# Turning three more things with the DMA engines in a one-core decoder step: the prompt's stick-breaking weights, its memory weights and the new sample values

## The chip, the cores and the metric

The kernel runs on one core of a Trainium2 chip. Five engines work side by side, each strictly in the order of its own queue: TensorE (PE: products; its weight loads are PEld), VectorE (DVE), ScalarE (ACT), GpSimd (POOL) and SyncE (SP), which here issues nearly all transfers to 16 DMA engines. The metric is the device time of one execution in microseconds (us), the median over several runs; lower is better.

## The reference, cut to what matters

One layer of a decoder with three branches beside each other, for 256 prompt tokens and 8 samples of 4 new tokens (288 columns in all). Two of the branches matter here, and of these the prompt's part:

```
# memory: 4 heads, 256 memory tokens
s = einsum('bqhd,bmhd->bhqm', q, k) * (HEAD_DIM ** -0.5)
p = softmax(s, axis=-1)
y = einsum('bhqm,bmhd->bqhd', p, v)
# stick-breaking: 8 heads, blocks of 128 queries, strictly causal
z = einsum('bqhd,bkhd->bhqk', q, k) * (HEAD_DIM ** -0.5) + b_sb
log_keep = where(causal, log_sigmoid(-z), 0.0)
after = cumsum(log_keep, axis=3, reverse=True) - log_keep
a = where(causal, exp(log_sigmoid(z) + after), 0.0)
y = einsum('bhqk,bkhd->bqhd', a, v)
```

The weights `p` and `a` come out with a query on each partition. The product with the values needs them with a key on each partition, so each 128x128 block is transposed ("turned") first. For two blocks of 128 queries a memory head has four such blocks; a stick-breaking head has three, as the fourth is all zeros. The samples' branch needs its new values `v` with a token on each partition: one block for each group of four heads.

## The kernel before, in words

Everything is kept with features on partitions and tokens in columns. The weights stream in as 504 slabs of 128x1024 numbers (512 KB). Each slab lands in one of four buffers `wr` (line 287), ACT rounds it to a coarse part `wh` (line 309), DVE makes the remainder `wl` (line 320), and PE multiplies: 24 products of 128x288 for a slab (line 516, in parts of six), with `wh` twice and `wl` once. `wh` and `wl` have four buffers each.

After the memory's own keys and values and the convolution's projections, PE takes the projections of the 4 memory heads and then of the 8 stick-breaking heads (key, query, values). The attention of each head is done beside these projections, as small jobs: `mem_rest(h)` for a memory head and `sb_head(h)` for a stick-breaking head. Between them they use the tile pools `s` (8 buffers of 128x512), `a` (75) and the PSUM pool `pa` (3). In `mem_rest` the scores are six products (`three`, lines 903 to 905), `softmax_rows` normalises them (line 923 last), four transposes on PE turn them (line 965), ACT and DVE split them in two parts (970, 972), and six more products with the values follow, again lines 903 to 905. In `sb_head` the scores are four products (line 1193 and `three`), a chain of ACT and DVE steps ends in the causal mask (line 1217), three transposes turn the weights (1221), ACT and DVE split them (1225, 1227, 1229), and `three` and line 1235 multiply them with the values. Each fourth head also turns `vs`, the new sample values, on PE (1187) and copies them to `vn` (1189), which `sb_sample` reads later.

One thing was turned by DMA already: the prompt's values, in `turned`. [...]

The order of all work is set before the kernel runs by a planner, `Order.run`. Each job is a Python generator that asks for an engine with an estimate (`act(n)`: 0.22 + n / 1200 us) and with what it needs: flags and buffers. The planner takes what can start earliest, and among such the smallest rank; the projections in `main` have rank 20 and fill every gap on PE. A step that changes engine is planned 0.15 us and a slack later (0.8 us for PE and SP, 0.1 us for the others). A landing is planned by `landed(kb)`: 1.2 us after the issue or after the transfers before it, then kb / 340 us, then 0.8 us. `turned` added 3.0 us to that. On the chip nothing of this is a clock: each engine works through its row as fast as the semaphores let it.

Of the kernel before, what the change touches and what calls it, by code (L numbers as in the profile page):

```python
# [75 lines left out]
class Order:  # L76
# [31 lines left out]
    def give(self, pool, n=1):  # L108
        self.pools[pool] += [self.now.ready] * n
# [49 lines left out]
def act(n, *flags, **take):  # L159
    return Ask("ACT", 0.22 + n / 1200.0, flags, **take)  # L160
# [6 lines left out]
def pe(us, *flags, **take):  # L167
    return Ask("PE", us, flags, **take)


def sp(*flags, **take):
    return Ask("SP", 0.45, flags, **take)
# [11 lines left out]
def tile_decoder_step(ctx: ExitStack, tc: tile.TileContext, xT, memT, wall, cvec, kmat, ptab,  # L184
# [23 lines left out]
    def tl(p, shape, dt=F32):  # L208
        cnt[0] += 1
        return pools[p].tile(shape, dt, tag=p, name=f"{p}_{cnt[0]}")  # L210

    def bank(p):
        return tl(p, [P, 512])
# [297 lines left out]
        done(rm_done)  # L511


    def chunk(ps, todo, first, last):
        for i, (w, a) in enumerate(todo):
            nc.tensor.matmul(ps, w, a, start=(first and i == 0), stop=(last and i == len(todo) - 1))  # L516
# [425 lines left out]
    def mem_rest(h, q):  # L942
            if h == 0:
                yield pool(1024, k4=1)
                qmx.append(tl("k4", [P, MH, NB, NS]))
                nc.gpsimd.memset(qmx[0], 0.0)
            yield dve(NS, *([qm_made[0]] if h else []))
            spread(nc, qmx[0][:, h], q[:, NP:])
            done(qm_made[h])
            qq = Pair()  # L950
            yield from split(qq, q[:, :NP], NP)
            give("a")
            yield pe(0.71, mk_done[h], *([om_made[h - 1]] if h else []), pa=1, s=1)
            s = bank("pa")
            for a in range(2):
                three(s[:, a * ML:(a + 1) * ML], qq, mk[h], slice(a * P, (a + 1) * P), slice(0, ML))
            give("a", 4)
            p = tl("s", [P, 512])
            yield from softmax_rows(s, 2, p)
            give("pa")  # L960
            yield pe(0.5, pa=1)
            tp = bank("pa")
            for m in range(2):
                for a in range(2):
                    nc.tensor.transpose(tp[:, m * NP + a * P:m * NP + (a + 1) * P],  # L965
                                        p[:, a * ML + m * P:a * ML + (m + 1) * P], ident)
            yield act(512, s=2)
            w = Pair()
            w.h, w.l = tl("s", [P, 512], F32R), tl("s", [P, 512], F32R)
            nc.scalar.copy(w.h, tp)  # L970
            yield dve(512)
            nc.vector.tensor_sub(w.l, tp, w.h.bitcast(F32))
            give("pa")
            give("s")
            yield pe(0.71, mv_done[h], pa=1)
            o = bank("pa")[:, :NP]
            for m in range(2):
                three(o, mv[h][m], w, slice((h % 2) * HD, (h % 2 + 1) * HD), slice(m * NP, (m + 1) * NP), m == 0, m == 1)
            give("s", 2)
            if h % 2:  # L980
                give("a", 4)
            yield act(NP, a=2)
            omem[h] = Acts()
            nc.scalar.copy(omem[h].h[:, :NP], o)
            yield dve(NP)
            nc.vector.tensor_sub(omem[h].l[:, :NP], o, omem[h].h[:, :NP].bitcast(F32))
            give("pa")
            done(om_made[h])
# [165 lines left out]

    def turned(h, v, vt):

        yield act(4 * P, a=1)
        x = tl("a", [P, T])[:, :NP].bitcast(U16)
        nc.scalar.copy(x.rearrange("p (x t) -> p x t", x=2), v[:, :NP].bitcast(U16).rearrange("p (t x) -> p x t", x=2))
        yield sp(a=1)  # L1160
        y = tl("a", [P, T])[:, :NP].bitcast(U16)
        nc.sync.dma_start_transpose(y.rearrange("p (c d) -> p c d", c=4), x)
        here = Flag()
        here.at = order.landed(131) + 3.0
        yield act(4 * P, here, a=1)
        f = tl("a", [P, T])
        nc.scalar.copy(f[:, :NP].bitcast(U16).rearrange("p (t x) -> p x t", x=2), y.rearrange("p (x t) -> p x t", x=2))
        give("a", 3)
        yield from split(vt, f[:, :P], P)
        vt.raw = f[:, P:NP]  # L1170
        done(v_made[h])

    def sb_head(h):
        def evac(ps):
            yield dve(T, rx_done, a=1)
            v = tl("a", [P, T])
            nc.vector.tensor_mul(v, ps, rx)
            give("pm")
            add(store(oV[h], v), 3)
            yield act(NS)  # L1180
            nc.scalar.copy(vs[:, h % 4 * NS:(h % 4 + 1) * NS], v[:, NP:])
            vt = Half()
            add(turned(h, v, vt), 2.25 + 0.05 * h)
            if h % 4 == 3:
                yield pe(0.11, pa=1)
                tp = bank("pa")[:, :P]
                nc.tensor.transpose(tp, vs, ident)
                yield act(P)
                nc.scalar.copy(vn[:, h // 4, :], tp)
                give("pa")  # L1190
            yield pe(0.54, k_made[h], q_made[h], pa=1, s=3)
            zp = bank("pa")[:, :384]
            nc.tensor.matmul(zp[:, 0:128], qs_[h].raw[:, 0:P], ks[h].raw[:, 0:P], start=True, stop=True)  # L1193
            three(zp[:, 128:384], qs_[h], ks[h], slice(0, P), slice(0, NP))
            give("a", 5)
            z, l, sp_ = (tl("s", [P, 512]) for _ in range(3))
            yield act(384)
            nc.scalar.activation(z[:, :384], zp, AF.Identity, scale=SCALE, bias=col(C_BSB + h))
            give("pa")
            zz, ll, ss = z[:, :384], l[:, :384], sp_[:, :384]  # L1200
            yield from softplus_parts(zz, ll)
            yield dve(384)
            nc.vector.scalar_tensor_tensor(ss, zz, 0.0, ll, op0=ALU.max, op1=ALU.add)
            yield dve(256)
            nc.vector.tensor_mul(blocks2(sp_, P), blocks2(sp_, P), twice(caus, P))
            yield dve(384)
            nc.vector.scalar_tensor_tensor(zz, zz, 0.0, ll, op0=ALU.min, op1=ALU.subtract)
            yield dve(2 * 384)
            nc.vector.tensor_tensor_scan(ll[:, ::-1], ones_s[:, :384][:, ::-1], ss[:, ::-1], 0.0,
                                         op0=ALU.mult, op1=ALU.add)  # L1210
            yield dve(384)
            nc.vector.tensor_sub(zz[:, :383], zz[:, :383], ll[:, 1:])
            give("s")
            yield act(384)
            act_fn(LN_EXP, zz, zz, AF.Exp)
            yield dve(256)
            nc.vector.tensor_mul(blocks2(z, P), blocks2(z, P), twice(caus, P))
            yield pe(0.35, pa=1)
            tp = bank("pa")[:, :384]
            for i in range(3):  # L1220
                nc.tensor.transpose(tp[:, i * P:(i + 1) * P], z[:, i * P:(i + 1) * P], ident)  # L1221
            yield act(256, s=2)
            w, raw = Pair(), tl("s", [P, 512])
            w.h, w.l = (lambda x: (x[:, :256], x[:, 256:]))(tl("s", [P, 512], F32R))
            nc.scalar.copy(w.h, tp[:, :256])
            yield act(P)
            nc.scalar.copy(raw[:, :P], tp[:, 256:])
            yield dve(256)
            nc.vector.tensor_sub(w.l, tp[:, :256], w.h.bitcast(F32))
            give("pa")  # L1230
            give("s", 2)
            yield pe(0.54, v_made[h], pa=1)
            op = bank("pa")[:, :NP]
            three(op, vt, w, slice(0, P), slice(0, NP), last=False)
            nc.tensor.matmul(op[:, P:NP], vt.raw, raw[:, :P], start=False, stop=True)  # L1235
            give("s", 2)
            give("a", 2)
            yield act(NP, a=2)
            a = osb[h] = Acts()
            nc.scalar.copy(a.h[:, :NP], op)  # L1240
            yield dve(NP)
            nc.vector.tensor_sub(a.l[:, :NP], op, a.h[:, :NP].bitcast(F32))
            give("pa")
            done(osb_made[h])
        return evac

    def sb_sample(g):
# [37 lines left out]
        def new_values():  # L1285
            yield pool(P, t=1)
            e = tl("t", [P, T])[:, :P]
            nc.gpsimd.memset(e, 0.0)
            for i in range(4):
                yield dve(NS)  # L1290
                c = slice(i * NS, (i + 1) * NS)
                nc.vector.transpose(e[c, c], z[c, NP:T])
            box.append(e)

        def first(ps):
            nc.tensor.matmul(ps, box[0], vn[:, g, :], start=True, stop=False)
# [384 lines left out]
```

## Time and profile before

| | |
|---|---|
| median of 3 runs | 1625.31 us (1625.14 to 1625.55) |
| profiled execution, its own time | 1625.22 us |
| its span, first to last instruction | 1623.4 us |
| busy: PE / DVE / ACT / POOL | 1618.8 / 1003.6 / 738.8 / 138.3 us |
| granted clock of PE | 1.00 |

"Busy" is the time in which an engine executed something. The profile's chain that ended last follows the work back from the last instruction; its lines say which engine and which line of the kernel held the end at each moment. Tile names are those of the pools, with numbers left out. The heads' attention lies between about 137 and 357 us of the span.

### The profile page before, as it was taken

What the parts mean: (1) busy time and instruction counts of PE and PEld (TensorE: products, weight loads), DVE (VectorE), ACT (ScalarE), POOL (GpSimd) and SP (SyncE); (2) the same over time, 40 slices, a digit from 0 to 9 for tenths busy, and PEclk for the clock granted to TensorE, in tenths of its full rate; (3) what the DMA queues carried; (4) which work ended last, traced back from release to release, by engine and by line L of the source; (5) the groups of instructions that cost most, each with busy time, mean ns of one, the idle gap of its engine ahead of it and who ended that gap; (6) DMA issues with size and microseconds to landing.
All of it is one profiled execution on the core that took longest, in us unless ns stands there. A gap on an engine that the chain in (4) does not pass through costs nothing.

```text
span 1623.4 us, 30845 instructions
## 1 busy us (share of the span) xinstructions
PE 1618.8 (100%) x12713; PEld 1603.1 (99%) x12713; DVE 1003.6 (62%) x1493; ACT 738.8 (46%) x1068; POOL 138.3 (9%) x107
## 2 busy tenths in 40 slices
PE   9999999999999999999999999999999999999999
PEld 7999999999999999999999999999999999999999
DVE  8899898877777755665555544555445544455543
ACT  8746766654433544444443333333333333333332
POOL 0020000000000000002222100121001210022100
PEclk9999999999999999999999999999999999999999
DMA  9787465788755555556655555555555555555662
GB/s 337 216 187 267 141 178 177 255 287 298 266 179 173 167 170 169 168 176 193 195 171 170 170 169 170 167 169 169 170 168 168 170 170 168 171 168 169 181 191 101
DMA packets 111454, 306.36 MB, mean 189 GB/s; under 512 B 24274, under 2 KB 33874, under 8 KB 111314
## 3 DMA queue, kind: packets, MB, share of 16 engines
q1 hardware_dynamic: 111170, 304.38, 60.0%
q8 instruction: 99, 1.62, 0.4%
q14 instruction: 41, 0.34, 0.1%
q10 hardware_dynamic: 144, 0.02, 0.0%
HBM read 296.99 MB, written 6.32 MB: 187 GB/s over the span
## 4 chain that ended last, share of the span: by engine, by line
PE 100%; POOL 0%; DVE 0%; issue 0%; POOLq 0%
PE pm L516 93%; PE pm L569 3%; PE pa L516 1%; PE pl L1070 1%; PE pl L1259 0%; PE pa L903 0%; PE pa L905 0%; PE pa L904 0%; PE pl L1084 0%; PE pa L1477 0%; PE pa L1221 0%; PE pa L1193 0%; PE pa L965 0%; PE pa L1235 0%; PE pa L863 0%; PE pa L663 0%
## 5 line engine op out<-in xcount | busy, mean ns | idle before, releaser
L309 ACT CAST wh<-wr 128x1024 fp32r<-128x1024 f32 (+1 forms) x520 | 530.4, 1023 | 633.1 <-PE pm L516 569.3
L516 PE MATMUL pm<-a,wh 128*128 128x288 f32 x5184 | 738.5, 293 | 0.0
L320 DVE TENSOR_TENSOR wl<-wr,wh 128x1024 fp32r<-128x1024 f32 (+1 forms) x520 | 620.0, 1195 | 191.1 <-ACT wh L309 187.8
L516 PEld LDWEIGHTS pm<-a,wh 128*128 128x128 f32 x5184 | 695.9, 188 | 1.0 <-issue 1.0
L516 PE MATMUL pm<-a,wl 128*128 128x288 f32 x2592 | 397.9, 292 | 0.0
L516 PEld LDWEIGHTS pm<-a,wl 128*128 128x128 f32 x2592 | 358.2, 188 | 0.2 <-issue 0.2
L516 PE MATMUL pm<-k,wh 128*128 128x288 f32 x2400 | 338.1, 292 | 0.0
L516 PEld LDWEIGHTS pm<-k,wh 128*128 128x128 f32 x2400 | 321.1, 188 | 0.0
L516 PE MATMUL pm<-k,wl 128*128 128x288 f32 x1200 | 182.1, 292 | 0.0
L516 PEld LDWEIGHTS pm<-k,wl 128*128 128x128 f32 x1200 | 165.2, 188 | 0.0
L1414 POOL TENSOR_TENSOR t<-t 128x288 f32<-128x288 f32 x64 | 95.5, 1494 | 600.5 <-DVE t L1411 600.5
L1428 DVE TENSOR_TENSOR a<-a,pm 128x288 f32<-128x288 f32 x64 | 29.1, 454 | 122.4 <-PE pm L516 122.4
L1411 DVE SCALAR_TENSOR_TENSOR t<-pm,rx 128x288 f32<-128x288 f32 x64 | 29.2, 457 | 90.8 <-PE pm L516 90.8
L1417 ACT CAST k<-t 128x288 fp32r<-128x288 f32 x60 | 25.9, 433 | 123.3 <-POOL t L1414 123.3
L1330 DVE TENSOR_TENSOR t<-pm,rx 128x288 f32<-128x288 f32 x48 | 22.0, 458 | 68.1 <-PE pm L516 68.1
L1419 DVE TENSOR_TENSOR k<-t,k 128x288 fp32r<-128x288 f32 x60 | 27.8, 465 | 58.3 <-ACT k L1417 58.3
L747 DVE SCALAR_TENSOR_TENSOR a<-a,cv,a 128x256 f32<-128x256 f32 x120 | 57.5, 480 | 1.4
L1400 POOL TENSOR_TENSOR t<-t,t 128x288 f32<-128x288 f32 x15 | 21.6, 1443 | 387.6 <-ACT t L1397 387.6
L569 PE MATMUL pm<-wh,a 128*128 128x512 f32 x128 | 35.0, 395 | 0.0
L516 PE MATMUL pm<-s,wh 128*128 128x288 f32 x160 | 33.9, 292 | 0.0
L569 PEld LDWEIGHTS pm<-wh,a 128*128 128x128 f32 x128 | 24.3, 191 | 5.7 <-ACT wh L309 0.7
L516 PEld LDWEIGHTS pm<-s,wh 128*128 128x128 f32 x160 | 25.4, 188 | 0.0
(209 smaller groups left out, 738.3 us busy)
## 6 DMA issues: line engine op xcount, KB each, us to landing
wr<-in_wall SPq DMA_DIRECT2D x488, 512.0 KB, 3.6
wr<-in_wall SPq DMA_DIRECT2D x32, 256.0 KB, 4.8
k<-in_kpool SPq DMA_DIRECT2D x32, 256.0 KB, 6.0
k<-in_vpool SPq DMA_DIRECT2D x32, 256.0 KB, 6.0
k<-in_mkc SPq DMA_DIRECT2D x8, 512.0 KB, 8.5
k<-in_mvc SPq DMA_DIRECT2D x8, 512.0 KB, 7.9
t<-in_xT SPq DMA_DIRECT2D x16, 144.0 KB, 3.5
out_yT<-a SPq DMA_DIRECT2D x16, 144.0 KB, 1.8
```

What stands on the lines that cost most here:

```text
L309: nc.scalar.copy(sl.h[:, c], sl.raw[:, c])
L320: nc.vector.tensor_sub(sl.l[:, c], sl.raw[:, c], sl.h[:, c].bitcast(F32))
L516: nc.tensor.matmul(ps, w, a, start=(first and i == 0), stop=(last and i == len(todo) - 1))
L569: nc.tensor.matmul(ps[m], y[:, m * P:(m + 1) * P], z[:, w], start=(k == 0 and j < 2), stop=(k == KT - 1 and j in (4, 5)))
L747: nc.vector.scalar_tensor_tensor(c[:, :NP], up[:, k:k + NP], w, c[:, :NP], op0=ALU.mult, op1=ALU.add)
L1330: nc.vector.tensor_mul(g, ps, rx)
L1400: nc.gpsimd.tensor_add(sq_sum[0], sq_sum[0], res[0])
L1411: nc.vector.scalar_tensor_tensor(r, ps, 0.0, r2, op0=ALU.max, op1=ALU.mult)
L1414: nc.gpsimd.tensor_mul(r, r, r)
L1417: nc.scalar.copy(a.h, r)
L1419: nc.vector.tensor_sub(a.l, r, a.h.bitcast(F32))
L1428: nc.vector.tensor_add(x1[j], x1[j], ps)
```

## The change

A helper `turn(src, n, place, ...)` takes the three steps out of `turned`: ACT writes the planes, SP issues the DMA transpose, ACT joins the halfwords. `place` names the tiles to use. It plans 2.0 us, where `turned` had 3.0 us, after the landing. It is used for four things now:

- the prompt's values, as before (4 blocks of 128x128 halfwords for a head, 8 times);
- a memory head's weights (512 numbers in a row, 8 blocks, 4 times), instead of line 965;
- a stick-breaking head's weights (384 numbers, 6 blocks, 8 times), instead of line 1221. They end in the tile `ll`, so the copy of the third block (1227) is gone too;
- the new sample values (128 numbers, 2 blocks, twice), instead of lines 1187 and 1189, in a job of their own, `turned_new`, that writes `vn`.

The splits (970, 972, 1225, 1229) then read SBUF, where they read PSUM. `sb_head(4)` is planned after `vn` of the first group, and `sb_sample` after its own.

```diff
+    def turn(src, n, place, **take):
+
+        yield act(2 * n, **take)
+        x, y, out = place()
+        nc.scalar.copy(planes(x), halves(src))
+        yield sp()
+        nc.sync.dma_start_transpose(y.bitcast(U16).rearrange("p (c d) -> p c d", d=P), x.bitcast(U16))
+        here = Flag()
+        here.at = order.landed(n * P * 4 / 1e3) + 2.0
+        yield act(2 * n, here)
+        nc.scalar.copy(halves(out), planes(y))
+        return out
...
-            yield pe(0.5, pa=1)
-            tp = bank("pa")
-            for m in range(2):
-                for a in range(2):
-                    nc.tensor.transpose(tp[:, m * NP + a * P:m * NP + (a + 1) * P],
-                                        p[:, a * ML + m * P:a * ML + (m + 1) * P], ident)
+            def place():
+                x = tl("s", [P, 512])
+                return x, p, x
+
+            x = yield from turn(p, 512, place, s=1)
+            give("s")
             yield act(512, s=2)
             w = Pair()
             w.h, w.l = tl("s", [P, 512], F32R), tl("s", [P, 512], F32R)
-            nc.scalar.copy(w.h, tp)
+            x, wh = (y.rearrange("p (i j q) -> p i j q", i=2, j=2) for y in (x, w.h))
+            wh = wh.rearrange("p m a q -> p a m q")
+            nc.scalar.copy(wh, x)
             yield dve(512)
-            nc.vector.tensor_sub(w.l, tp, w.h.bitcast(F32))
-            give("pa")
+            nc.vector.tensor_sub(w.l.rearrange("p (m a q) -> p a m q", m=2, a=2), x, wh.bitcast(F32))
...
+    def turned_new(g):
+
+        def place():
+            x, y = (tl("a", [P, T])[:, :P] for _ in range(2))
+            return x, y, vn[:, g, :]
+
+        yield from turn(vs, P, place, a=2)
+        give("a", 2)
+        done(vn_made[g])
...
             if h % 4 == 3:
-                yield pe(0.11, pa=1)
-                tp = bank("pa")[:, :P]
-                nc.tensor.transpose(tp, vs, ident)
-                yield act(P)
-                nc.scalar.copy(vn[:, h // 4, :], tp)
-                give("pa")
+                add(turned_new(h // 4), 2.9)
...
-            yield pe(0.35, pa=1)
-            tp = bank("pa")[:, :384]
-            for i in range(3):
-                nc.tensor.transpose(tp[:, i * P:(i + 1) * P], z[:, i * P:(i + 1) * P], ident)
-            yield act(256, s=2)
-            w, raw = Pair(), tl("s", [P, 512])
+            yield from turn(zz, 384, lambda: (ll, zz, ll))
+            give("s")
+            yield act(256, s=1)
+            w = Pair()
             w.h, w.l = (lambda x: (x[:, :256], x[:, 256:]))(tl("s", [P, 512], F32R))
-            nc.scalar.copy(w.h, tp[:, :256])
-            yield act(P)
-            nc.scalar.copy(raw[:, :P], tp[:, 256:])
+            nc.scalar.copy(w.h, ll[:, :256])
             yield dve(256)
-            nc.vector.tensor_sub(w.l, tp[:, :256], w.h.bitcast(F32))
-            give("pa")
-            give("s", 2)
+            nc.vector.tensor_sub(w.l, ll[:, :256], w.h.bitcast(F32))
...
-            nc.tensor.matmul(op[:, P:NP], vt.raw, raw[:, :P], start=False, stop=True)
+            nc.tensor.matmul(op[:, P:NP], vt.raw, ll[:, 256:], start=False, stop=True)
```

The planner then writes other rows for every engine. Three places are shown. Lines are those of each kernel: 516, 903 to 905, 1193 and 1235 of before are 535, 922 to 924, 1214 and 1250 of the kernel after; 524, 526 and 530 are the three steps of `turn`.

PE of before, at the transposes of stick-breaking head 0 (`km` holds the identity, `pm` is the projection under way, `wh` the slab):

```order
L516 MATMUL pm_2633<-a_282,wh_2521 128x288
L516 MATMUL pm_2633<-a_283,wh_2521 128x288
L1221 MATMUL pa_2645<-km,s_2451 128x128 x3
L516 MATMUL pm_2633<-a_378,wh_2521 128x288
L516 MATMUL pm_2633<-a_379,wh_2521 128x288
```

The three transposes stand between products of a slab. PE of before, 24 products of the projection and four transposes later, at the same head's product with its values:

```order
L516 MATMUL pm_2633<-a_607,wh_2545 128x288
L903 MATMUL pa_2700<-s_2667,a_2325 128x256
L904 MATMUL pa_2700<-s_2667,a_2325 128x256
L905 MATMUL pa_2700<-s_2667,a_2325 128x256
L1235 MATMUL pa_2700<-s_2666,a_2316 128x128
L516 MATMUL pm_2633<-a_610,wh_2545 128x288
```

PE of the kernel after, at the same product (`s_2374` is now the tile `ll`):

```order
L535 MATMUL pm_2573<-a_511,wl_2531 128x288
L535 MATMUL pm_2573<-a_544,wl_2531 128x288
L922 MATMUL pa_2667<-s_2637,a_2318 128x256
L923 MATMUL pa_2667<-s_2637,a_2318 128x256
L924 MATMUL pa_2667<-s_2637,a_2318 128x256
L1250 MATMUL pa_2667<-s_2374,a_2197 128x128
L535 MATMUL pm_2573<-a_606,wl_2531 128x288
```

Between the head's first score product and its first product with the values PE had 120 projection products in its row, and has 156 now. For memory head 3, the same count goes from 84 to 114; for the other ten heads it grows by 12 (where 64 small products of the samples come between as well) to 120.

SP of before, around the values of stick-breaking head 1 (`wr` is a slab, `out_oK` and `out_oV` are outputs):

```order
L678 DMA out_oK<-a_2357 128x288
L287 DMA wr_2417<-in_wall 128x1024
L678 DMA out_oV<-a_2441 128x288
L287 DMA wr_2466<-in_wall 128x1024
L1162 DMA_TRANSPOSE a_2481<-a_2455 128x4x128
L287 DMA wr_2523<-in_wall 128x1024
L287 DMA wr_2560<-in_wall 128x1024
```

SP of the kernel after, at the same values:

```order
L287 DMA wr_2416<-in_wall 128x1024
L697 DMA out_oV<-a_2419 128x288
L526 DMA_TRANSPOSE s_2364<-s_2437 128x8x128
L526 DMA_TRANSPOSE a_2468<-a_2467 128x4x128
L287 DMA wr_2497<-in_wall 128x1024
L287 DMA wr_2529<-in_wall 128x1024
L526 DMA_TRANSPOSE s_2373<-s_2374 128x6x128
L287 DMA wr_2549<-in_wall 128x1024
```

The weights of memory head 1 (`s_2364`) and of stick-breaking head 0 (`s_2373`) are turned on each side of the values' transpose, with slabs behind them. ACT of before, from the split of head 0's turned weights on:

```order
L1225 CAST s_2667<-pa_2645 128x256
L1227 COPY s_2666<-pa_2645 128x128
L845 ACTIVATE t_2627<-t_2626 128x288
L845 ACTIVATE t_2641<-t_2640 128x288
L309 CAST wh_2689<-wr_2523 128x1024
L970 CAST s_2705<-pa_2683 128x512
```

ACT of the kernel after, at the landing of head 0's weights:

```order
L309 CAST wh_2571<-wr_2416 128x1024
L309 CAST wh_2589<-wr_2497 128x1024
L1004 CAST a_2604<-pa_2582 128x256
L226 ACTIVATE t_2395<-pa_2594,eps 128x288
L226 ACTIVATE t_2395<-t_2395 128x288
L871 CAST t_2510<-t_2509 32x288
L530 COPY s_2374<-s_2373 128x2x384
L1244 CAST s_2637<-s_2374 128x256
```

Where ACT had waited for PE's transposes, it now waits at line 530 for a landing, and what stands behind it in its row, slabs too, waits with it.

More of the change, by code (lines that the diff above doesn't have):

```diff
@@ L511, in mem_norm, with planes, halves @@
         done(rm_done)
+    def planes(x):
+        return x.bitcast(U16).rearrange("p (x t) -> p x t", x=2)
+    def halves(x):
+        return x.bitcast(U16).rearrange("p (t x) -> p x t", x=2)
+    def turn(src, n, place, **take):
[9 more added lines that the diff above has]
+        return out
     def chunk(ps, todo, first, last):
@@ L1155, in turned, with place @@
     def turned(h, v, vt):
[L1157 to L1170, printed above, removed]
-        done(v_made[h])
+        def place():
+            x, y = (tl("a", [P, T])[:, :NP] for _ in range(2))
+            return x, y, x
+        x = yield from turn(v[:, :NP], NP, place, a=2)
+        give("a", 2)
+        yield from split(vt, x[:, :P], P)
+        vt.raw = x[:, P:]
+        done(v_made[h])
+    def turned_new(g):
+        def place():
+            x, y = (tl("a", [P, T])[:, :P] for _ in range(2))
+            return x, y, vn[:, g, :]
+        yield from turn(vs, P, place, a=2)
+        give("a", 2)
+        done(vn_made[g])
+    vn_made = [Flag(), Flag()]
     def sb_head(h):
@@ L1179, in evac @@
             add(store(oV[h], v), 3)
-            yield act(NS)
+            yield act(NS, *([vn_made[0]] if h == 4 else []))
             nc.scalar.copy(vs[:, h % 4 * NS:(h % 4 + 1) * NS], v[:, NP:])
@@ L1293, in new_values @@
             box.append(e)
+            yield dve(0, vn_made[g])
         def first(ps):
```

## Prediction

> **What bounds the kernel now.** I read the page first, its busy times and its chain of waits, then that chain in order of time around the edit, then one row of engine times over the stretch of the heads.
>
> ```profile
> span 1623.4 us, 30845 instructions
> PE 1618.8 (100%) x12713; PEld 1603.1 (99%) x12713; DVE 1003.6 (62%) x1493; ACT 738.8 (46%) x1068; POOL 138.3 (9%) x107
> ...
> PEclk9999999999999999999999999999999999999999
> ...
> PE 100%; POOL 0%; DVE 0%; issue 0%; POOLq 0%
> ```
>
> PE carries the whole chain, at full granted clock; of 1623.4 us it is busy 1618.8. So any PE instruction that goes away shortens the span by its own pitch, as long as PE never waits for what replaces it. The chain in order of time gives that pitch, since each piece there lasts until the next begins:
>
> ```profile
> 144.25 0.44 PE pa L965 x4
> ...
> 159.87 0.59 PE pa L965 x4
> ...
> 188.11 0.33 PE pa L1221 x3
> ...
> 188.44 2.35 PE pm L516 x18
> ...
> 225.98 0.11 PE pa L1187
> ...
> 352.53 0.33 PE pa L1221 x3
> ```
>
> A transpose holds PE for 0.44 / 4 = 0.33 / 3 = 0.11 us, though its own record is longer; a product of a slab holds it for 2.35 / 18 = 0.1306 us.
>
> ```profile
> core 0: us, PE busy (x) PEld busy (x) DVE busy (x) ACT busy (x) POOL busy (x), PEclk, DMA share, GB/s
> 120.00:360.00 240.00, 240.00 (x2040) 236.10 (x2040) 211.64 (x390) 158.21 (x309) 4.91 (x6) 1.00 0.66 213
> ```
>
> In the stretch of the heads PE has no gap, ACT is busy 158.2 / 240 = 66%, DVE 88%, the DMA engines 66%. So ACT and DMA have room; DVE has little, but its row keeps its work.
>
> **The change, part by part.** PE loses 4 x 4 + 8 x 3 + 2 = 42 transposes: 42 x 0.11 = 4.62 us. (The one group at 0.59 us follows small products; I count its extra 0.15 us as theirs. With it the gain is 4.77 us.) Nothing is added on PE. This is the gain, all of it on the chain.
>
> ACT and DVE are priced from these rows (min/median/max in ns):
>
> ```profile
> L1159 ACT COPY a<-a x8: 602/614/616, 153.0 to 317.8; 128x512 uint16<-128x512 uint16 x8
> L1167 ACT COPY a<-a x8: 770/778/786, 162.7 to 326.6; 128x512 uint16<-128x512 uint16 x8
> L1181 ACT COPY vs<-a x8: 202/218/219, 152.9 to 317.6; 128x32 f32<-128x32 f32 x8
> L1225 ACT CAST s<-pa x8: 349/373/375, 189.1 to 352.9; 128x256 fp32r<-128x256 f32 x8
> L1227 ACT COPY s<-pa x8: 262/272/281, 189.3 to 353.2; 128x128 f32<-128x128 f32 x8
> L970 ACT CAST s<-pa x4: 586/588/589, 144.7 to 191.3; 128x512 fp32r<-128x512 f32 x4
> L1229 DVE TENSOR_TENSOR s<-pa,s x8: 414/420/426, 189.7 to 354.4; 128x256 fp32r<-128x256 f32 x8
> L972 DVE TENSOR_TENSOR s<-pa,s x4: 682/691/693, 146.1 to 193.3; 128x512 fp32r<-128x512 f32 x4
> ```
>
> Taking 0.22 us for a nearly empty copy (L1181) as the fixed part, 512 halfwords cost 0.39 us more to spread into planes and 0.56 us more to join. So a stick-breaking head (768 halfwords) pays 0.22 + 0.59 = 0.81 and 0.22 + 0.84 = 1.06 us, a memory head (1024) 1.01 and 1.34 us, the sample values (256) 0.42 and 0.50 us. Bounds for the largest: the times at 512 as they are, or doubled (0.61 to 1.23 and 0.78 to 1.56 us). Sum: 8 x 1.87 + 4 x 2.35 + 2 x 0.92 = 26.2 us, less 8 x 0.27 for line 1227 and 2 x about 0.27 for line 1189 (same shape): +23.5 us. ACT then stands at (158.2 + 23.5) / 240 = 76% of the stretch; I cost that at nothing, since PE's products cover it. The splits read SBUF in place of PSUM; I take the same durations, and a tenth either way is under 0.1 us on a path with the reserves below.
>
> SP issues 14 more transposes, 4 x 8 + 8 x 6 + 2 x 2 = 84 more blocks. The rows of the present ones, and one that followed the samples' pages:
>
> ```profile
> L1162 SPq DMA_TRANSPOSE a<-a x8: 1197/1204/1666, 153.6 to 318.4; - x8
> ...
> DMA to landing us min/median/max: 2.4/3.9/9.2
> ...
> 295.48 0.82 SPq L1035 DMA_DIRECT2D k<-in_mvc  x1
> 296.40 1.22 SPq L1162 DMA_TRANSPOSE a<-a  x1
> ...
> 248.50:249.50 1.00, 1.00 (x10) 1.00 (x9) 0.97 (x2) 0.98 (x2) 0.00 (x0) 1.00 0.48 86
> 249.50:250.50 1.00, 1.00 (x10) 1.00 (x9) 0.96 (x3) 0.12 (x1) 0.00 (x0) 1.00 0.77 111
> ```
>
> Issuing takes 1.20 / 4 = 0.30 us a block if each block is issued for itself, 25 us over the stretch, with slabs queued behind; bound below: 1.20 us whatever the size. In the two windows at 249 us, just after a transpose was issued, the DMA engines were busy 0.48 + 0.77 = 1.25 us, an estimate of one transpose; 84 blocks make 21 x 1.25 = 26 us, out of 240 x 0.34 = 82 us that are free. I cost both at nothing: PE's products cover them.
>
> What remains is latency. From issue to landing a transpose of 4 blocks took 3.9 us (median); with 0.30 us a block I take 4.5 us for 6 blocks and 5.1 us for 8 (bounds: 2.4 us, and 9.2 us behind a backlog of pages). Does PE reach the product with the values before its operand is there? The tightest places by the order are stick-breaking head 0 and memory head 3:
>
> ```profile
> 185.90 0.42 DVE L1217 TENSOR_TENSOR s<-s,km 128x256 f32<-128x256 f32 x1
> 189.66 0.42 DVE L1229 TENSOR_TENSOR s<-pa,s 128x256 fp32r<-128x256 f32 x1
> 191.85 0.28 PE L903 MATMUL pa<-s,a 128*128 128x256 f32 x1
> ...
> 188.25 0.89 ACT L923 ACTIVATE s<-s,sm 128x256 f32<-128x256 f32 x2
> ...
> 193.29 0.68 DVE L972 TENSOR_TENSOR s<-pa,s 128x512 fp32r<-128x512 f32 x1
> ...
> 196.34 0.28 PE L903 MATMUL pa<-s,a 128*128 128x256 f32 x1
> ```
>
> Head 0: its masked weights were ready at 186.32, and PE took them at 191.85, 5.53 us later; the split had ended at 190.08, so 1.77 us of that were reserve. The new way needs 0.81 + 4.5 + 1.06 + 0.37 + 0.42 = 7.2 us and hand-overs (estimate 0.4 us). PE's row has 36 more products in between (156 for 120) and 11 transposes less, those of two memory heads and its own: 36 x 0.1306 - 11 x 0.11 = 3.5 us more. 5.53 + 3.5 = 9.0 us are there for 7.6 us, if ACT and DVE come to the mask as early as before: a landing up to 5.9 us is free. Memory head 3: 196.34 - 189.14 = 7.2 us, and 114 products for 84, 6 transposes less and three 128x256 products more (0.12 us each) make 3.5 us more, 10.7 us. Needed: 1.01 + 5.1 + 1.34 + 0.59 + 0.69 + 0.4 = 9.1 us; a landing up to 6.7 us is free. By the same count every other head gains 5.5 to 20 us of cover. So typical landings hide, and a backlogged one at a tight head would not: I allow 0.2 us in all for PE's waits. The transposes of the sample values feed a product that comes tens of us later; no cost.
>
> [...]
>
> Sum against the profiled execution: 1625.22 - 4.62 + 0.2 = 1620.8 us. The median of the runs lies 0.09 us above that execution, so 1620.9 us.
>
> **The rivals.**
>
> A. Some landings come late, and PE waits at line 1250 or at a memory head's product. For it: the 9.2 us landing above, issued right behind a page of the samples; with two more blocks 9.8 us, 3.9 us over what head 0 has. Against it: the heads behind pages (4, 6 and 7) got 16 to 20 us of cover. One such wait: 1620.7 + 3.9 = 1624.6 us; two: 1628.5 us. It takes the gain back to within 0.2% (1622.1) from 1.4 us on.
>
> B. Slower: ACT, waiting in its row for landings, is late with the slabs, and PE waits for `wh` and `wl`.
>
> ```profile
> L320 DVE TENSOR_TENSOR wl<-wr,wh 128x1024 fp32r<-128x1024 f32 (+1 forms) x520 | 620.0, 1195 | 191.1 <-ACT wh L309 187.8
> ...
> L309 ACT CAST wh<-wr x67: 1032/1051/1066, 119.6 to 357.9; 128x1024 fp32r<-128x1024 f32 x67
> ...
> ACT wh L309 <- PE pm L516: 19.0, 16, 2.2
> ```
>
> For it: in the stretch only 16 of 67 casts waited for a buffer to come free, so most start later than they could. With four buffers of 24 x 0.1306 = 3.1 us, an early cast leads PE by 9.4 us, less 1.05 and 1.20 us for cast and remainder: 7.2 us of reserve at best, about half for a typical one (estimate: 3.6 us). If each of the 12 turned weights kept ACT 5.3 us longer than planned (9.2 - 3.9), each would cost PE 1.7 us: 1620.7 + 20 = 1641 us. It decides (above 1628.6) from 0.7 us for each turn. Against it: ACT has a third of its time free, and usual landings of 4 to 5 us lie within what the planner allows (1.2 + 0.6 + 0.8 + 2.0 us behind the issue's 0.45 us).
>
> C. The latency isn't hidden at all: PE waits out what the new way takes longer than the old one, which was 190.08 - 186.32 = 3.8 us for head 0 and 193.97 - 189.14 = 4.8 us for memory head 3, from mask or softmax to the end of the split. That is 8 x (7.6 - 3.8) + 4 x (9.1 - 4.8) = 48 us more, 1668 us. PE's order, with 12 to 120 further projection products in each gap, speaks against it. [...]
>
> **How the numbers follow.** Forecast 0.62, A 0.25, B 0.10, C 0.03. A measurement here can tell about 0.2%, 3.25 us, from no change. The forecast is faster by 4.4 us (0.27%), A falls within 0.2%, B and C are slower: 0.62, 0.25, 0.13. The lower end is the larger gain, 4.77 us, and a little for splits that read SBUF faster: 1619.8. The upper end takes in most of A, one late landing and a third of a second: 1626.0. What is left out above is the rest of A, B and C, about 0.2.
>
> **What would show it.** Right: PE's 42 transposes are gone from the chain, PE still carries 100% of it, and its busy time is 1614.2 us with the span 4.6 us shorter; ACT's busy time is 762 us; ACT waits for landings, for 1 or 2 us now and then, and PE doesn't. Wrong by A: rows in which PE waits for the DVE split (line 1229's place) or the memory heads' one; by B: PE waits for DVE at `wl` or ACT at `wh` between 140 and 380 us, and slabs land later behind the transposes on SP. A gain over 5.5 us would mean that the pitch of 0.11 us wasn't the whole price of a transpose.

## The result and the profile after

| | before | after |
|---|---|---|
| median | 1625.42 us (1625.00 to 1625.91, 12 runs) | 1621.60 us (1621.05 to 1622.10, 12 runs) |
| profiled execution, its own time | 1625.22 us | 1621.28 us |
| its span | 1623.4 us | 1619.5 us |
| ratio, 95% interval | | 0.9977 (0.9968 to 0.9985) |

The changed kernel is 3.8 us faster. The forecast was 1620.9 us, in a range of 1619.8 to 1626.0 us.

The page of the kernel after, its span, its busy times and the engines' shares of its chain:

```profile
span 1619.5 us, 30821 instructions
PE 1613.8 (100%) x12671; PEld 1597.6 (99%) x12671; DVE 1004.1 (62%) x1493; ACT 759.9 (47%) x1086; POOL 138.4 (9%) x107
...
PE 99%; DMA 0%; DVE 0%; SPq 0%; ACT 0%; issue 0%
```

PE has 42 instructions less and 5.0 us less busy time, ACT has 21 us more, and PE still carries the chain. What PE waited for, in all, in times and at the longest:

```profile
PE pa L1493 <- POOL eps L234: 1.3, 1, 1.3
PE pm L535 <- DVE t L1346: 0.6, 1, 0.6
PE pm L588 <- ACT wh L309: 0.4, 1, 0.4
```

None of these is at a product with turned weights. The first lies at the program's start, and the third, at line 588, ahead of 50 us, where no head has begun. The second is new and lies between the heads; the chain in order of time shows it (start, length, what):

```profile
294.01 4.71 PE pm L535 x36
298.71 0.02 issue
298.74 0.47 DVE t L1346
299.21 0.04 issue
299.25 4.17 PE pm L535 x30
...
828.27 787.81 PE pm L535 x6060
```

Line 1346 takes a gate's finished sum out of its PSUM bank. PE stood still for 0.53 us, from 298.71 to 299.25, until that was done. The last row holds everything from 828.27 us on. The chain of before has the same piece, with the same 6060 products and the same length, 4.07 us later, so the whole difference arose ahead of it:

```profile
122.18 0.13 PE pa L863
...
832.34 787.81 PE pm L516 x6060
```

The row at 122.18 is the same instruction as the first one here, of the kernel after:

```profile
121.99 0.13 PE pa L882
...
155.75 3.59 PE pl L1104 x64
159.34 0.33 PE pa L882
```

Up to there the two executions differ by 0.19 us. Between the two marks, the stretch that holds the heads, before took 832.34 - 122.18 = 710.16 us and after 706.28 us: 3.88 us less. The other two rows settle a small point: behind 64 of the samples' small products, line 882 takes 0.33 us instead of 0.13 us. The same chain has this surcharge behind other small products too: one product of line 922 takes 0.32 us at 307.12 instead of 0.12, and two of line 1214 take 0.42 us at 347.46 instead of 0.22. The four transposes at 0.59 us, instead of 0.44, had paid it in the kernel before. It didn't go away with them.

### The profile page after: what moved, and what is told of

Same layout as the page of the kernel before. It is cut to its first block, busy times and chain, and to the rows that moved or that the text cites. A ratio compares the mean times of both kernels' runs of the same rounds, so it can differ in the third digit from the quotient of the medians.

```text
span 1619.5 us, 30821 instructions
## 1 busy us (share of the span) xinstructions
PE 1613.8 (100%) x12671; PEld 1597.6 (99%) x12671; DVE 1004.1 (62%) x1493; ACT 759.9 (47%) x1086; POOL 138.4 (9%) x107
## 4 chain that ended last, share of the span: by engine, by line
PE 99%; DMA 0%; DVE 0%; SPq 0%; ACT 0%; issue 0%
PE pm L535 93%; PE pm L588 3%; PE pa L535 1%; PE pl L1090 1%; PE pl L1274 0%; DMA wr<-in_wall 0%; PE pa L922 0%; PE pa L924 0%; PE pa L923 0%; PE pl L1104 0%; PE pa L1214 0%; PE pa L1250 0%; PE pa L882 0%; PE pa L682 0%; PE pa L1038 0%; ACT wh L309 0%
```

## The experiments

Each ran beside the kernel before on the same chip, and ratios are against that. Medians of before were 1625.43 and 1625.47 us.

**The price of a transpose on PE.** The kernel before, with each of the 42 transposes issued twice.

```diff
-                    nc.tensor.transpose(tp[...], p[...], ident)
+                    for _ in range(2):
+                        nc.tensor.transpose(tp[...], p[...], ident)
...    (likewise at the stick-breaking heads and at the sample values)
```

> The kernel before, in its own order, with each of the 42 transposes issued twice on PE (the planner isn't told). My theory: a transpose costs PE its pitch, 0.11 us, and nothing is hidden, so 42 x 0.11 = 4.6 us more than before: 1630.0 us. Rival: part of a transpose's time lies under the neighbours' weight loads, and its real price is lower: under 3 us more, 1625.5 to 1628.4 us.

Measured: 1630.24 us (1629.46 to 1630.69), ratio 1.0029 (1.0018 to 1.0039), +4.81 us. Its chain in order of time:

```profile
144.47 0.88 PE pa L966 x8
...
189.66 0.65 PE pa L1224 x6
```

Eight transposes take 0.88 us and six 0.65 us. So 0.11 us is the price of one, and nothing is hidden about it: 42 more cost what the forecast said that 42 fewer would save, 4.62 us, within 0.2 us.

**The transposes back in, in the new order.** The kernel after, with 42 transposes of a constant tile on PE ahead of the products with the values. Everything else of the change stays.

```diff
-            op = bank("pa")[:, :NP]
+            op = bank("pa")
+            for i in range(4 if h % 4 == 3 else 3):
+                nc.tensor.transpose(op[:, NP + i % 2 * P:NP + (i % 2 + 1) * P], ones_s[:, P:2 * P], ident)
+            op = op[:, :NP]
...    (four likewise in each memory head)
```

> The kernel after, in its own order and with its DMA turns, with 42 dead transposes of 128x128 put back on PE, ahead of each product with the values (the planner isn't told; their result isn't used). My theory: the gain was PE's pitch, so 1621.6 + 4.6 = 1626.2 us, 0.8 us over the kernel before; that 0.8 us is then the price of the new order, most of it the 0.5 us wait for a pm bank at 298.7 us of the profile. Rival: PE loses time at the turned weights' landings; dead work in front of the waiting product would fill such waits, and the time would be under 1625.4 us.

Measured: 1626.20 us (1625.67 to 1626.54), ratio 1.0005 (0.9996 to 1.0013). That is 4.60 us over after, again 42 x 0.11. What remains over before, 0.77 us by the medians, is what the other order and the new waits cost; by the interval alone it could be nothing, but the two chains above say nearly the same of the heads, 4.62 - 3.88 = 0.74 us. One of PE's waits in it:

```profile
...
PE pm L535 <- DVE t L1352: 0.6, 1, 0.6
```

The 0.6 us wait for the gate's bank is there too (line 1352 is 1346 moved down), so it belongs to the order and not to the missing transposes.

**More work on ACT.** The kernel after, with the copy into planes (one halfword of each number to the first plane, the other to the second) done twice for the 12 turned weights: +10.8 us of ACT's time by the copies' durations. ACT's busy time grew by 9.8 us (769.7 against 759.9).

```diff
-        nc.scalar.copy(planes(x), halves(src))
+        for _ in range(2 if src.shape[-1] in (384, 512) else 1):
+            nc.scalar.copy(planes(x), halves(src))
```

> The kernel after, in its own order, with the first copy (planes) of each turned weight done twice on ACT: 8 x 0.83 + 4 x 1.05 = 10.8 us more of ACT, and each turn 0.8 to 1.05 us later (the planner isn't told). My theory: reserves of 1.6 us and more cover it, 1621.6 us within 0.4 us. Rival (ACT or the landing is at the edge): PE waits at several of the 12 products or for slabs, 1 to 10 us more.

Measured: 1621.44 us (1621.18 to 1621.89), ratio 0.9975 (0.9965 to 0.9984): no change from after. Half as much ACT work again as the change had added costs nothing, so the 21 us that it did add were hidden with room to spare.

**Late landings, in two sizes.** The kernel after, with four, and in a second kernel ten, stores of 144 KB put on SP ahead of each of the 12 weight transposes. They write to memory that nobody reads.

```diff
+        for _ in range(4 if src.shape[-1] in (384, 512) else 0):      # 10 in the second kernel
+            nc.sync.dma_start(scratch[at_scratch[0]], km)
+            at_scratch[0] += 1
         nc.sync.dma_start_transpose(...)
```

> The kernel after, in its own order, with four stores of a 144 KB table to a scratch in HBM issued by SP ahead of each of the 12 transposes of weights (the planner isn't told). Each landing comes about 1.7 us later (4 x 0.34 us of issue, 4 x 0.42 us of DMA). My theory: in the profile of the kernel after ACT comes to the landed weights 5.4 us or more after the issue against landings of 4.2 us (median), and the split is done 0.9 to 2.8 us ahead of PE, so nearly all of it is covered: 1621.6 to 1623 us. Rival: the latency is bare, and 12 x 1.7 us are added: 1642 us.

> As the run with four stores, with ten: each landing 3.4 to 4.3 us later than in the kernel after. My theory: that is past the slack of about half the 12 turns, ACT waits at the landing, and PE waits 1 to 2 us at some products or for slabs: 1624 to 1636 us, so slower than the kernel before or near it. Rival (a landing never matters): 1621.6 us.

Four stores: 1621.41 us (1621.21 to 1621.64), ratio 0.9976 (0.9966 to 0.9985), no change. Of the weights' turns (`s<-s`), by line, with durations in ns and the first and last start, the kernel after has

```profile
L526 SPq DMA_TRANSPOSE s<-s x12: 1215/1238/4559, 144.5 to 367.5; - x12
L526 SPq DMA_TRANSPOSE a<-a x10: 1173/1196/2597, 154.9 to 311.9; - x10
...
DMA to landing us min/median/max: 2.4/4.2/12.3
```

and the kernel with four stores, of its weights and values together,

```profile
DMA to landing us min/median/max: 2.9/4.7/8.1
```

with ACT's waits for transfers of it

```profile
ACT s L536 <- DMA s<-s: 2.9, 4, 1.2
ACT a L536 <- DMA a<-a: 1.0, 1, 1.0
```

Landing by landing, the twelve weights came 0.0 to 2.6 us later than in the kernel after (median 1.9, where 1.7 were expected). The time of issue alone does not tell this: the first weights were issued at 148.6 in place of 144.5, but took 8.1 us to land in place of 12.3, so they were there at the same time, 156.8 and 156.7. In the kernel after ACT had come to landed weights 0.4 to 4.5 us after their landing. Now it waited for landings, 3.9 us in five places, which it never did in the kernel after. PE did not: its waits are those of after but for the 0.4 us one at `wh`. ACT's row and PE's each had a reserve, and the one of PE was not used up.

Ten stores: 1646.46 us (1645.57 to 1650.18), ratio 1.0137 (1.0122 to 1.0153), 24.9 us slower than after and 10 us over the end of what was expected. Measured against the product that PE had under way, the weights landed 2.4 to 8.0 us later than in the kernel after (median 5.0, where 3.4 to 4.3 were expected; eleven of the twelve landings are recorded). PE's waits that the kernel after has not:

```profile
PE pa L928 <- ACT s L1250: 6.7, 4, 3.0
PE pa L928 <- ACT s L997: 5.5, 2, 3.8
...
PE pa L929 <- DVE s L999: 0.7, 2, 0.3
```

PE waited 12.9 us in these, and all of it at the products with the values, which is rival A's place. But the weights' landing was not always what came late. ACT waited 24.6 us for the weights' landings, and it waited 38.1 us for slabs at line 309, against 22.0 us in the kernel after: the stores hold up the slabs behind them too. At two places ACT stood at the cast of a slab, with the joining of the halfwords behind it in its row:

```profile
162.02 1.05 ACT L309 CAST wh<-wr 128x1024 fp32r<-128x1024 f32 x1 [5.48 <-DMA wr<-in_wall]
...
320.93 1.05 ACT L309 CAST wh<-wr 128x1024 fp32r<-128x1024 f32 x1 [4.80 <-DMA wr<-in_wall]
```

Behind them PE waited 1.97 us near 165 and 2.95 us near 322. Ahead of PE's waits of 1.21, 3.84 and 1.95 us, near 195, 235 and 338, it was the weights that ACT had waited for (2.1, 5.0 and 3.5 us). So this run shows that late transfers cost much, by both ways; what late weights alone would cost it does not separate.

Nearly half of the loss is not a wait at all. The place of the second slab, in windows of 2 us (PE's busy time is the second number, the granted clock the one ahead of the last two):

```profile
320.00:322.00 2.00, 0.46 (x17) 0.19 (x7) 0.00 (x0) 1.07 (x2) 0.00 (x0) 1.00 1.06 406
322.00:324.00 2.00, 0.51 (x2) 0.32 (x2) 1.84 (x3) 1.33 (x2) 0.00 (x0) 0.92 1.02 408
324.00:326.00 2.00, 2.00 (x9) 2.00 (x10) 0.69 (x2) 1.55 (x2) 0.00 (x0) 0.50 1.03 409
326.00:328.00 2.00, 2.00 (x14) 2.00 (x13) 1.83 (x4) 1.97 (x6) 0.00 (x0) 0.73 0.35 91
328.00:330.00 2.00, 2.00 (x18) 2.00 (x17) 1.85 (x5) 1.97 (x7) 0.00 (x0) 1.00 0.85 222
```

PE stands still for 2.95 us, and then, busy again, runs at a granted clock of 0.50: 9 products fall in that window, and 18 in the last, at 1.00. PE's busy time grew by 1624.5 - 1613.8 = 10.7 us though it did the same work, and its time without work by 13.5 us; together that is the span's 24.2 us. There are four such drops of the clock (near 167, 238, 324 and 340 us). At the first, 24 products of line 541 took 4.69 us in the chain, and at the last 33 took 5.88 us; at 0.1306 us each they would have taken 3.13 and 4.31 us. Four times that difference, an estimate from these two, explains some 6 us of the 10.7. The rest lies in the first products behind each wait: near 196 us, where the clock stayed full, the second came 0.46 us after the first (rows in the last section), where the pitch is 0.12 us. Start by start against the kernel after, the two add up to the 10.7 us within a few tenths.

**The allowance behind a landing.** The kernel after, planned with 1.0 us behind a landing in place of 2.0. The instructions are the same, in other rows.

```diff
-        here.at = order.landed(n * P * 4 / 1e3) + 2.0
+        here.at = order.landed(n * P * 4 / 1e3) + 1.0
```

> The kernel after, with 1.0 us instead of 2.0 us planned behind a landing. Every engine does the same instructions; only their order differs. Theory that the order around the heads' end is worth more than the change itself (PE waits for the four pm banks there, since DVE, busy 87%, takes the last heads' projections out late): PE waits several us, 1626 to 1632 us. Rival that only the instructions on PE count: 1621.6 us within 0.6 us.

Measured: 1631.10 us (five of six runs from 1630.36 to 1631.37; one at 8949 us, unlike any other here, is not explained), ratio 1.0032 (1.0020 to 1.0045): slower than before, by one wait. Its row, and the chain around it:

```profile
PE pm L535 <- DVE a L1203: 8.1, 1, 8.1
```

```profile
275.06 8.59 PE pm L535 x66
...
292.99 0.59 ACT s L1219
...
299.56 0.43 DVE s L1238
...
300.50 0.47 DVE a L1203
...
301.02 6.85 PE pm L535 x30
```

PE had run out of PSUM banks for its next projection. Line 1203 takes a head's values out of a bank; in DVE's row it stood behind the chain of ACT and DVE steps that makes another piece of weights, and PE waited through all of that. Then 30 products took 6.85 us, 0.228 us each, where 66 had taken 8.59 us, 0.130 us each. In windows of 2 us the granted clock was 0.50 from 298 to 306 us and 0.79 in the next, so 2.9 us were lost at the lower clock on top of the wait. No DMA appears in the chain here: the landings weren't the cause.

**The values taken out first.** That kernel once more, with one thing changed: for stick-breaking heads 6 and 7 the step that takes the values out of their bank gets a higher rank in the planner, and keeps it until the bank is free.

```diff
     def give(self, pool, ...):
+        if pool == "pm" and self.now.then is not None:
+            self.now.rank = self.now.then
...
-            yield from main_tile(hx, sb_head(h), 2.2 + 0.05 * h)
+            yield from main_tile(hx, sb_head(h), 2.2 + 0.05 * h, 2, 1.0 if h in (6, 7) else None)
```

> The kernel with 1.0 us planned behind a landing (1631.1 us), in which the planner gives DVE's first step of the value projections of stick-breaking heads 6 and 7 (out of the pm bank) rank 1.0 in place of 2.5 and 2.55. The instructions are those of the kernel after. My theory: the 8.1 us that PE waited for a pm bank came from that step standing in DVE's row behind a head's serial chain of DVE and ACT; with it ahead PE never waits there: 1621.0 us, 0.5 us under the kernel after and 10 us under the kernel with 1.0 us. Rival: DVE is simply full at the heads' end, and another bank or slab is late instead: 1626 to 1632 us.

Measured: 1620.88 us (1620.51 to 1621.13), ratio 0.9972 (0.9962 to 0.9983), 10.2 us under the last kernel. When the two heads' values left their banks, with the lower allowance alone and here (the last two numbers ahead of the semicolon; in the kernel after they were 283.1 and 303.8):

```profile
L1203 DVE TENSOR_TENSOR a<-pm,rx x2: 457/457/457, 300.5 to 302.2; 128x288 f32<-128x288 f32 x2
```

```profile
L1208 DVE TENSOR_TENSOR a<-pm,rx x2: 458/458/458, 272.1 to 291.6; 128x288 f32<-128x288 f32 x2
```

They left 11 to 28 us earlier, and PE doesn't wait for a bank any more. All of its waits in this kernel:

```profile
PE pa L1498 <- POOL eps L239: 1.3, 1, 1.3
```

The chain of this kernel, at the two marks used above:

```profile
121.81 0.13 PE pa L887
...
827.41 787.81 PE pm L540 x6060
```

The same stretch took 705.60 us, 4.56 us less than before. So with the wait for the bank gone, the 42 transposes are worth nearly the whole of their 42 x 0.11 = 4.62 us. The work and the lower allowance are those of the last kernel, and ACT waited for landings in both; so it was the written order that made the 8.1 us wait.

**Eight more.** The last kernel, planned with 1.5 us behind a landing, and with the memory's keys for the prompt turned by DMA as well: 8 transposes less on PE.

```diff
-            for i in range(2):
-                for m in range(MT):
-                    nc.tensor.transpose(tp[...], raw[m][:, h * HD:(h + 1) * HD], ident)
...
+        for m in range(MT):
+            def place():
+                x = tl("s", [P, MW])
+                return x, raw[m], x
+            cols.append((yield from turn(raw[m], MW, place, s=1)))
```

> The former kernel with 1.5 us planned behind a landing, and with the memory's prompt keys turned by DMA too: 8 transposes less on PE, 2 turns more, 8 copies of 128 columns on ACT for 4 of 256. My theory: 8 x 0.11 = 0.9 us less than the former: 1620.1 us. Rival: at the memory stage ACT and DVE are fuller (busy 80 to 90%) and the first slabs tight, so PE waits there: 1621 to 1626 us.

Measured: 1620.03 us (1619.67 to 1620.13), ratio 0.9967 (0.9955 to 0.9979): 0.85 us under the last kernel for 8 x 0.11 = 0.88 us of work, and the fastest of all kernels here, 1.6 us under the changed one. Two things differ from the last kernel, the keys and the allowance, and no run has the allowance of 1.5 us alone. In the chains the two groups of four transposes, 0.44 us each in the last kernel, are gone; the products ahead of them took 0.42 us longer (44.94 against 44.52), so that the two profiled spans differ by 0.7 us.

## Why the prediction was right

- **What bounds the kernel.** PE's row does, before and after, and PE's pitch is what counts. Twice the transposes (+4.81 us), the transposes back in (+4.60 us) and eight fewer still (-0.85 us) give 0.115, 0.110 and 0.106 us for each, against the 0.11 us taken from the chain. These are differences of medians whose runs scatter by some tenths of a us, so the third, of eight transposes alone, is rough.
- **The gain.** 4.62 us were forecast, 3.88 us came in the heads, and 4.56 us do in the kernel without the new wait. The 4.77 us at the range's low end did not come: the dearer group's 0.15 us belonged to the small products ahead of it, and passed on to line 882. Nor did splits that read SBUF faster: ACT's took 406 and 622 ns (256 and 512 columns, medians of lines 1244 and 991), against 373 and 588 ns from PSUM, and DVE's 420 and 692 ns (1246 and 993), against 420 and 691.
- **The allowance for PE's waits** was the term that was mis-sized: 0.2 us forecast, about 0.7 us found (4.62 - 3.88), of which 0.53 us is one row. It was also placed wrongly. I had looked for it at the products with the values, behind a landing; it came at a PSUM bank that DVE had not yet emptied, since the planner had written DVE's row anew. No part of the sum covered what a new order does to the banks, and the lower allowance shows that this could have cost 10 us: a result slower than before by a mechanism that none of the rivals had.
- **ACT.** +21.1 us measured, +23.5 forecast. Hidden, as forecast; the doubled copies are hidden too. The copies that were scaled from smaller ones (min/median/max in ns, first and last start) took

```profile
L524 ACT COPY s<-s x12: 826/829/1047, 142.4 to 359.4; 128x768 uint16<-128x768 uint16 x8, 128x1024 uint16<-128x1024 uint16 x4
L530 ACT COPY s<-s x12: 1060/1081/1374, 159.0 to 374.5; 128x768 uint16<-128x768 uint16 x8, 128x1024 uint16<-128x1024 uint16 x4
```

  so 0.83 and 1.05 us to spread (0.81 and 1.01 forecast) and 1.07 and 1.37 us to join (1.06 and 1.34).
- **Issue and landing.** The 0.30 us a block was wrong, and its lower bound right: issuing took 1.2 us for 2, 4, 6 or 8 blocks alike (medians of 1.24 us for 6 and 8 blocks, 1.20 us for 2 and 4; rows of line 526 above). Landings were 4.2 us in the median. Three of the weights' landings took 12.3, 11.0 and 9.4 us (memory head 0, stick-breaking heads 4 and 6), as long as the one that rival A was made from, and nobody waited for them: ACT came to them 2.2 us or more after they had landed. I had expected ACT to wait 1 or 2 us for a landing now and then; it never did.
- **The tight places.** Head 0, from the masked weights to the product:

```profile
175.87 0.42 DVE L1238 TENSOR_TENSOR s<-s,km 128x256 f32<-128x256 f32 x1
...
178.84 1.97 SPq L526 DMA_TRANSPOSE s<-s  x1
...
185.83 1.06 ACT L530 COPY s<-s 128x768 uint16<-128x768 uint16 x1
...
187.36 0.42 DVE L1246 TENSOR_TENSOR s<-s,s 128x256 fp32r<-128x256 f32 x1 [0.19 <-ACT s L1244]
...
189.65 0.28 PE L922 MATMUL pa<-s,a 128*128 128x256 f32 x1
```

  The split was done at 187.78 and PE came at 189.65: 1.87 us of reserve, where 9.0 - 7.6 = 1.4 us were forecast. That these two are close is luck. The mask was ready at 176.29, so 13.4 us were there, and the steps took 11.5 us of them; each is some 4 us more than forecast. Part of it is that ACT came to the weights 1.9 us after they had landed, a second reserve that the forecast did not have. Over the twelve heads the reserve ahead of PE was 0.94 to 2.81 us. It was least at memory head 0, and not at the two heads forecast as tightest; the 5.5 to 20 us of cover that the other heads gained in PE's row did not show as reserve there. (For memory head 3 the forecast's sum of 30 products, 6 transposes and 3 products gives 3.6 us, not 3.5.)
- **Rival A** did not come. With landings 0.0 to 2.6 us later PE still lost nothing; with landings some 5 us later, and slabs late as well, PE waited there, and then it is dearer than worked out: the forecast counted waits alone, and PE's busy time grew by nearly as much again (10.7 us, against 13.5 us without work), by the lower clock and by slow products behind each wait. Where between the two a late landing begins to cost is open. **Rival B** did not come either: ACT's casts waited longer for slabs (22.0 us in all against 15.1), but PE lost nothing at `wh` or `wl` in the heads. Under the ten stores late slabs did cost, but at the products with the values, through ACT's row, and not at `wh` or `wl`. **Rival C** would have PE wait at the products with the values, and in the kernel after it waited at none. The way by DMA is the longer one, 1.2 us for the issue alone and 4.2 us in the median to landing, where three blocks on PE took 0.33 us; but here the longer way was covered, and 0.11 us of PE a block was not.

## What to carry to other kernels

Where one engine carries the chain without a gap, price what you take off it by its pitch in the chain (0.11 us for a transpose here), not by its record (0.27 us), and price what replaces it by whether the next user comes later than it does. Then ask of a written order what stands in front of each step that frees a buffer: here the same instructions in another order cost 10 us, more than twice what the change was worth. Five waits of 1.95 to 8.1 us on TensorE cost more than their length here, since products behind them ran at a granted clock of about 0.5.

## What the hardware showed that I had not expected

The granted clock dropped behind waits as short as 1.95 us. Two more places of the kernel with ten stores, each with a product of PE and the idle time ahead of it, and then with windows of 2 us:

```profile
165.00 0.38 PE L928 MATMUL pa<-s,a 128*128 128x256 f32 x1 [1.63 <-ACT s L997]
```

```profile
166.00:168.00 2.00, 2.00 (x13) 2.00 (x13) 1.88 (x6) 1.78 (x4) 0.00 (x0) 0.66 0.86 311
168.00:170.00 2.00, 2.00 (x10) 2.00 (x9) 1.90 (x5) 1.21 (x6) 0.00 (x0) 0.50 0.70 270
```

```profile
195.97 0.39 PE L928 MATMUL pa<-s,a 128*128 128x256 f32 x1 [1.21 <-ACT s L1250]
196.43 0.39 PE L929 MATMUL pa<-s,a 128*128 128x256 f32 x1
```

```profile
196.00:198.00 2.00, 1.93 (x13) 1.73 (x14) 1.97 (x5) 1.93 (x5) 0.00 (x0) 1.00 1.03 420
```

In the first place 1.97 us without work (the 1.63 us, and 0.34 us behind that one product) were followed by a clock of 0.50; in the second, 1.21 us were not, and the clock stayed at 1.00. The run's other three drops came behind 4.19 us without work (3.84 and 0.35, near 235), 2.95 us (near 322) and 1.95 us (near 338). The lowest clock of a 2 us window behind these was 0.56, 0.50 and 0.50.

How long a drop lasted can be estimated from the windows. At the first place the shares that are missing from full clock, 0.34 + 0.50, and 0.02 in the window behind them, of windows of 2 us, make 0.86 x 2 / 0.5 = 3.4 us at half the clock, and the three rows of the place at 324 above 0.08 + 0.50 + 0.27, also 3.4 us, if the clock was 0.50 throughout. What decides whether a wait is followed by a drop was not shown.

The issue of a DMA transpose took 1.2 us (median) whatever its size from 2 to 8 blocks, so here 8 blocks in one transpose held the issuing queue no longer than 2 did.
